# Gate block 6's negated half and adding DMA come first, and even heads of the indexer's last two row blocks take their PSUM bank from the values' pool

## The chip, the cores and the metric

The kernel runs on one core of a Trainium2 chip. The metric is the device time of one execution in microseconds (us). Before the change it was 752.59, 752.68 and 753.98 us in three runs, so the median is 752.68.

## The reference

The program computes one block of a streaming encoder for 512 frames of 1024 channels, in fp32. A projection feeds two attention branches with eight heads of 64 each; gates merge them; a layer norm, a gated feed-forward layer (width 2816, with a causal convolution of width 3) and a second layer norm follow.

```python
proj = x @ w_in
q_a, k_a, v_a, q_i, k_i, w_i, q_s, k_s, v_s, g_a, g_b = split(proj)

# branch A (heads a0..a7): an indexer picks the 128 best keys of a query
dots  = einsum('thd,sd->ths', q_i, k_i) * 64**-0.5        # 8 indexer heads, one key head
score = einsum('th,ths->ts', w_i, relu(dots))             # masked to earlier chunks
sel   = top_k(score, 128)                                 # 128 = min(256, 512 // 4)
y_a   = softmax(q_a . k_a[sel] / 8 + bias) @ v_a[sel]

# branch B (heads s0..s7): stick breaking, no softmax
log_beta, log_keep = log_sigmoid(z), log_sigmoid(-z)      # z = q_s . k_s / 8, causal
y_s   = exp(log_beta + sum of log_keep over later keys) @ v_s

merged = sigmoid(g_a + b_a) * (y_a @ w_dsa) + sigmoid(g_b + b_b) * (y_s @ w_sb)
x = layer_norm(alpha * x + merged @ w_out)
u, g = split(x @ w_ffn_in)
x = layer_norm(alpha * x + (gelu(conv(u)) * g) @ w_ffn_out)
```

## The kernel before, in words

**Products in three matmuls.** Each fp32 operand of a projection is split in a high half and a low half, and a product is the sum of three matmuls into one PSUM bank. In the projections (`proj_t`) these are the lines L230 (high weights, high x), L231 (high weights, low x) and L232 (low weights, high x). A projection of 128 output channels has 8 such triples, 24 matmuls of 128x512.

**The weight stream.** The class `Stream` brings the weights in the order in which the matmuls use them. SP's queue loads a raw block (128x1024, L72) a few blocks ahead; ACT writes the high half `whi` (L103); the low half `wlo` is raw minus high. For most blocks DVE or POOL subtracts (L110). For the fourteen blocks in `DMA_LO`, gate blocks gb0 to gb7 among them, ACT writes the *negated* high half into `wlo` (L106), and then a DMA that POOL issues reads the raw weights from memory a second time and adds them to it (L107). `whi` and `wlo` are rings of three blocks each, so that a block may be written only when the matmuls of the block three places earlier are done. The numbers in the names count the blocks: `wlo_29` belongs to gb5, `wlo_30` to gb6, `wlo_31` to gb7, `whi_32` to qa1.

**Filler and heads.** The list `FILL` is the order of the projections: ... qa0 ka0 gb4 gb5 gb6 gb7 qa1 ka1 va ... (q, k and v of the branches, gates of branch B). They are cut into triples and put between the steps of the attention heads, which have waits in them. The heads go s0 to s7, then a0 to a7. For an s head, TensorE forms z (L530), ACT takes the two sigmoids (L534 and L535, tiles `keep` and `beta`), DVE scans `keep` (L544), and POOL multiplies `beta` by the scan (`sb_sticks`, L547). Tiles `beta_1524`, `beta_1642` and `beta_1773` belong to heads 5, 6 and 7. The result has to be transposed before it meets the values. From head 4 on (`TURN = 4`) that is done by DMA: `send_planes` splits the fp32 words into two 16-bit planes (L466 on ACT, L467 on POOL), SP issues two transposing DMAs (L469), and `join_planes` puts the planes together (L478 on ACT, L479 on POOL) and writes high and low halves (`pth` L481 on ACT, `ptl` L485 on DVE). TensorE reads both in `weigh` (L501).

**The indexer.** `idx_scores` walks over row blocks 1, 2 and 3 (256, 384 and 512 keys) and eight heads in each: two matmuls into a PSUM tile `dot_ps` (L403, L404), a relu on ACT (L406), and on DVE a product with the head's weight that adds to the score (L409, L411). The selection (`select`, L420 and L421 on DVE) is a long row of rounds, dealt out between the later steps.

**PSUM.** There are two pools of four banks. `pa` serves the projections and the indexer's dots; `pb` serves the values' projection (`vs_ps0` to `vs_ps3`), and after it the heads.

**What sets the order.** Each engine runs its instructions in a fixed order. A scheduler, which times the program when it is built, sets that order; `tc.issue_after(x)` makes what is written under it come after x in that plan. Ahead of the change the multiply of head 5 (L547, `i == TURN + 1`) came after the last adding DMA written so far (`st.added`); the multiply of head 6 had no such tie.

## Time and profile before

| | |
|---|---|
| time, median of three runs | 752.68 us |
| the profiled execution | 753.88 us, of which the span of the trace is 752.1 us |
| granted TensorE clock over the span | 0.994 |
| PE (TensorE matmul) busy | 739.6 us, 98% |
| DVE (VectorE) busy | 569.3 us, 76% |
| ACT (ScalarE) busy | 406.4 us, 54% |
| POOL (GpSimd) busy | 149.5 us, 20% |
| queue 1 (transfers that SP's and ACT's queues issue) | 41.1% of 16 DMA engines' span |
| queue 0 (transfers that POOL issues) | 9.7% |

All times are microseconds from the start of the span. PE is the matrix engine's matmuls, PEld its weight loads, DVE the vector engine, ACT the scalar engine, POOL the GpSimd engine, SP the queue that issues most transfers. In a row of the timeline stand the start, the duration, the engine, the line, the operation and the tiles (out<-in, without numbers); in square brackets the time for which the engine stood idle before it, and what it waited for. Matmuls overlap: one is listed with 0.39 us, but the next starts 0.23 us after it. The clock column (PEclk) is the share of full speed that the chip granted to TensorE.

### The profile page before, as it was taken

The numbers are of one execution on the slowest core, as the hardware profiler recorded it, in microseconds if no ns is written. First come the engines' busy times: TensorE is split into PE (matmuls) and PEld (weight loads), VectorE is DVE, ScalarE is ACT, GpSimd is POOL, SyncE is SP. The second block draws the span as 40 slices with busy tenths as digits, with TensorE's granted clock in tenths as the row PEclk, the third lists the DMA queues.
The fourth block names the chain that finished last, engine by engine and source line by source line (L and its number), as shares of the span: only waits on it lengthen the run. The fifth ranks groups of instructions, "written<-read, shape, count | busy, mean of one in ns | idle before, by whom it ended". The sixth has DMA issues, their size and how long they took to land.

```text
span 752.1 us, 9760 instructions
## 1 busy us (share of the span) xinstructions
PE 739.6 (98%) x3485; PEld 619.5 (82%) x3485; DVE 569.3 (76%) x907; ACT 406.4 (54%) x572; POOL 149.5 (20%) x161
## 2 busy tenths in 40 slices
PE   9999999998999999999999999999999999999995
PEld 7877888886888888888889888888888888888885
DVE  5569788998579999658774967676776668668995
ACT  5465767795786588746374534443443344346430
POOL 1001224374742432000011111011101101110011
PEclk9999999999999999999999999999999999999998
DMA  8445887796556455327732444435343444448532
GB/s 268 151 127 183 190 183 170 151 203 162 133 152 161 122 146 118 121 61 231 303 60 75 170 143 158 146 114 167 125 159 136 140 141 143 141 146 290 198 117 84
DMA packets 71008, 116.38 MB, mean 155 GB/s; under 512 B 39913, under 2 KB 40169, under 8 KB 70961
## 3 DMA queue, kind: packets, MB, share of 16 engines
q1 hardware_dynamic: 63680, 93.33, 41.1%
q0 software_dynamic: 5744, 18.38, 9.7%
q10 hardware_dynamic: 1536, 4.06, 2.2%
q8 instruction: 27, 0.44, 0.3%
q14 instruction: 21, 0.16, 0.1%
HBM read 95.93 MB, written 9.98 MB: 141 GB/s over the span
## 4 chain that ended last, share of the span: by engine, by line
PE 92%; DVE 4%; DMA 1%; issue 1%; ACT 1%; POOL 0%; DVEq 0%; POOLq 0%; ACTq 0%
PE u_ps L922 5%; PE u_ps L921 5%; PE g_ps L922 5%; PE u_ps L923 5%; PE g_ps L921 5%; PE g_ps L923 5%; PE m L1002 2%; PE m L1001 2%; PE m L1003 2%; PE av_ps L501 2%; PE ga_ps L232 2%; PE ga_ps L231 2%; PE ga_ps L230 2%; PE o_ps L852 2%; PE o_ps L851 2%; PE o_ps L850 2%
## 5 line engine op out<-in xcount | busy, mean ns | idle before, releaser
L103 ACT ACTIVATE whi<-raw 128x1024 fp32r<-128x1024 f32 (+1 forms) x124 | 124.0, 1002 | 158.7 <-PE g_ps L922 45.9
L110 DVE TENSOR_TENSOR wlo<-raw,whi 128x1024 fp32r<-128x1024 f32 (+1 forms) x105 | 124.3, 1185 | 40.4 <-ACT whi L103 39.5
L923 PE MATMUL u_ps<-x1h,wlo 128*128 128x512 f32 (+1 forms) x192 | 71.4, 372 | 0.0
L921 PE MATMUL u_ps<-x1h,whi 128*128 128x512 f32 (+1 forms) x192 | 71.3, 372 | 0.0
L922 PE MATMUL u_ps<-x1l,whi 128*128 128x512 f32 (+1 forms) x192 | 71.3, 371 | 0.0
L921 PE MATMUL g_ps<-x1h,whi 128*128 128x512 f32 (+1 forms) x184 | 69.9, 380 | 0.0
L922 PE MATMUL g_ps<-x1l,whi 128*128 128x512 f32 (+1 forms) x184 | 69.9, 380 | 0.0
L923 PE MATMUL g_ps<-x1h,wlo 128*128 128x512 f32 (+1 forms) x184 | 69.9, 380 | 0.0
L921 PEld LDWEIGHTS u_ps<-x1h,whi 128*128 128x128 f32 x192 | 36.2, 188 | 6.3
L922 PEld LDWEIGHTS u_ps<-x1l,whi 128*128 128x128 f32 x192 | 36.2, 188 | 6.2
L923 PEld LDWEIGHTS u_ps<-x1h,wlo 128*128 128x128 f32 x192 | 36.2, 188 | 6.2
L921 PEld LDWEIGHTS g_ps<-x1h,whi 128*128 128x128 f32 x184 | 34.6, 188 | 6.6
L923 PEld LDWEIGHTS g_ps<-x1h,wlo 128*128 128x128 f32 x184 | 34.6, 188 | 6.5
L922 PEld LDWEIGHTS g_ps<-x1l,whi 128*128 128x128 f32 x184 | 34.6, 188 | 6.5
L944 DVE TENSOR_TENSOR t<-raw 128x512 f32<-128x512 f32 x11 | 7.6, 692 | 40.0 <-DMA raw<-in_w_fo_dram 39.6
L559 POOL TENSOR_TENSOR bm<-win,score 128x256 f32<-128x256 f32 (+2 forms) x24 | 26.0, 1112 | 32.2 <-DMA pl<-bm 16.1
L963 POOL MEMSET u<- 128x2 f32 x22 | 2.1, 98 | 145.0 <-ACT whi L103 101.2
L977 DVE TENSOR_TENSOR hF<-g_ps,c 128x512 f32<-128x512 f32 x22 | 15.1, 686 | 20.8 <-PE g_ps L923 20.8
L969 ACT ACTIVATE c<-c,cwt 128x512 f32<-128x512 f32 x22 | 15.9, 725 | 25.2 <-DVE c L968 25.0
L819 POOL TENSOR_TENSOR rstd<-rstd,mhalf 128x1 f32<-128x1 f32 x8 | 7.7, 958 | 104.4 <-DVE rstd L818 104.4
L232 PE MATMUL gb_ps<-xh,wlo 128*128 128x512 f32 x64 | 25.7, 404 | 2.6 <-DMA wlo<-in_w_t_dram 2.6
L420 DVE MAX8 m<-score 128x8 f32<-128x256 f32 (+2 forms) x48 | 26.5, 554 | 1.7 <-DMA pl<-keep 0.8
(578 smaller groups left out, 2085.2 us busy)
## 6 DMA issues: line engine op xcount, KB each, us to landing
raw<-in_w_fi_dram SPq DMA_DIRECT2D x44, 512.0 KB, 3.3
raw<-in_w_t_dram SPq DMA_DIRECT2D x32, 512.0 KB, 3.5
raw<-in_w_fo_dram SPq DMA_DIRECT2D x26, 512.0 KB, 4.1
wlo<-in_w_t_dram POOLq DMA_DIRECT2D x14, 512.0 KB, 7.1
raw<-in_w_br_dram SPq DMA_DIRECT2D x8, 512.0 KB, 4.0
raw<-in_w_o_dram SPq DMA_DIRECT2D x8, 512.0 KB, 4.4
raw<-in_w_v_dram SPq DMA_DIRECT2D x7, 512.0 KB, 3.8
raw_b<-in_w_fo_dram SPq DMA_DIRECT2D x6, 512.0 KB, 5.3
```

Source lines behind the costliest of these rows:

```text
L103: self.high = nc.scalar.activation(hi[:, :w], t[:, :w], AF.Copy).ins
L110: self.done[key] = eng.tensor_sub(lo[:, :w], t[:, :w], r32(hi[:, :w])).ins
L230: nc.tensor.matmul(ps[:M], wh[:, c], xh[k], start=(k == 0), stop=False)
L231: nc.tensor.matmul(ps[:M], wh[:, c], xl[k], start=False, stop=False)
L232: nc.tensor.matmul(ps[:M], wl[:, c], xh[k], start=False, stop=(k == KC - 1))
L420: nc.vector.max(m8, sc)
L559: nc.gpsimd.tensor_add(bm[:, OFF[j]:OFF[j] + N], win[:, 512 - N:512], score[j])
L921: nc.tensor.matmul(ps[:, c], wh[:, kc], x1h[:, k, c], start=(k == 0), stop=False)
L922: nc.tensor.matmul(ps[:, c], wh[:, kc], x1l[:, k, c], start=False, stop=False)
L923: nc.tensor.matmul(ps[:, c], wl[:, kc], x1h[:, k, c], start=False, stop=(k == KC - 1))
L969: nc.scalar.activation(c, c, AF.Gelu_apprx_tanh, bias=cwt[:, f, 3:4])
L977: nc.vector.tensor_mul(F[:, o:o + 2].rearrange("p a b -> p (a b)"), gps_, c)
```

## The change

1. For gb6 the negated half (L106) comes in ACT's order straight behind the block's high half. In the code, the high half of the next block, the two copies of ka0 (`stack_hl`, L335 and L336) and the sigmoid of gb4 (L627) are ordered behind it; ka0's copies had been ordered behind head 4's joined high half before.
2. The multiply of head 6 (L547) comes behind gb6's adding DMA in POOL's order; the one of head 5 comes behind gb5's, by name.
3. In row blocks 2 and 3 of the indexer, heads 0, 2, 4 and 6 take their PSUM bank from `pb`, the others from `pa` as before.

```diff
@@ -64,6 +64,7 @@
         self.loaded, self.split, self.used = {}, {}, 0
         self.nl = self.ns = 0
         self.high = self.behind = None
+        self.highs = {}
 
     def queue(self, dst, src):
 
@@ -103,8 +104,10 @@
                 self.high = nc.scalar.activation(hi[:, :w], t[:, :w], AF.Copy).ins
             self.behind = None
             if key in self.lo_by_dma:
-                self.high = nc.scalar.activation(lo[:, :w], r32(hi[:, :w]), AF.Copy, scale=-1.0).ins
-                self.done[key] = self.added = nc.gpsimd.dma_start(lo[:, :w], self.pieces[self.ns][1], accum_op=ALU.add).ins
+                self.high = self.highs[key] = nc.scalar.activation(lo[:, :w], r32(hi[:, :w]), AF.Copy, scale=-1.0).ins
+                if key == "gb6":
+                    self.behind = self.high
+                self.done[key] = nc.gpsimd.dma_start(lo[:, :w], self.pieces[self.ns][1], accum_op=ALU.add).ins
             else:
                 eng = nc.gpsimd if key in self.lo_on_pool else nc.vector
                 self.done[key] = eng.tensor_sub(lo[:, :w], t[:, :w], r32(hi[:, :w])).ins
@@ -398,7 +401,7 @@
             N = 128 * (j + 1)
             for h in range(H):
                 yield j
-                ps = pa("dot_ps")
+                ps = (pb if j > 1 and h % 2 == 0 else pa)("dot_ps")
                 r = slice(j * 128, j * 128 + 128)
                 nc.tensor.matmul(ps[:, :N], qi[h][:, r], kih[:, :N], start=True, stop=False)
                 nc.tensor.matmul(ps[:, :N], qi[h][:, r], kil[:, :N], start=False, stop=True)
@@ -535,7 +538,7 @@
             ups[h] = nc.scalar.activation(beta[:, c], ps[:, :o], AF.Sigmoid, scale=0.125).ins
         return beta, keep
 
-    def sb_sticks(beta, keep, behind=False):
+    def sb_sticks(beta, keep, behind=None):
 
         for j in (1, 0, 2, 3):
             N = 128 * (j + 1)
@@ -543,7 +546,7 @@
             rev = keep[:, hi:lo:-1]
             scan = nc.vector.tensor_tensor_scan(rev, rev, first[:, 512 - N:512][:, ::-1], 0.0, op0=ALU.mult,
                                                 op1=ALU.max)
-        with tc.issue_after(st.added) if behind else nullcontext():
+        with tc.issue_after(st.done[behind]) if behind else nullcontext():
             nc.gpsimd.tensor_mul(beta, beta, keep[:, 1:ATT + 1])
         return scan.ins
 
@@ -620,11 +623,12 @@
             if kind in ("qs", "qa"):
                 qk[t] = stack_dup(ps, 1.0 if kind == "qs" else -0.125, t)
             elif kind in ("ks", "ka"):
-                with tc.issue_after(firsts[0]) if t == "ka0" and firsts else nullcontext():
+                with tc.issue_after(st.highs["gb6"]) if t == "ka0" and firsts else nullcontext():
                     qk[t] = stack_hl(ps, "k", 4, t)
             elif kind == "gb":
                 g = xp.tile([128, 512], F32, tag="m", bufs=8, name=t)
-                ups[t] = nc.scalar.activation(g, ps, AF.Sigmoid, bias=bgt[:, 8 + n:9 + n]).ins
+                with tc.issue_after(st.highs["gb6"]) if n == 4 else nullcontext():
+                    ups[t] = nc.scalar.activation(g, ps, AF.Sigmoid, bias=bgt[:, 8 + n:9 + n]).ins
                 m.append(g)
             elif n >= EARLY:
                 gps[n] = ps
@@ -707,7 +711,7 @@
                 for ins in emptied["va"] if h == 2 else ends if h == 1 else ():
                     ties.enter_context(tc.issue_after(ins))
                 return following[0]()
-        last = sb_sticks(*following, behind=i == TURN + 1)
+        last = sb_sticks(*following, behind={TURN + 1: "gb5", TURN + 2: "gb6"}.get(i))
         if i < TURN:
             return following[0], last
         return send_planes(*following, nc.gpsimd), last
```

The scheduler makes a new order out of this. Lines of the changed kernel are one to four higher than those of before (L103 is L104, L106 is L107, L107 is L110, L335 is L338, L403 is L406, L466 and L467 are L469 and L470, L481 is L484, L547 is L550, L627 is L631).

ACT, where gb6's weights are split; `whi_30` and `wlo_30` are gb6's halves, `whi_31` and `wlo_31` gb7's, `ka0a` and `ka0b` the copies of ka0, `back_1718` the joined planes of head 5, `keep_1643` a plane of head 6. Before:

```order
L103 ACTIVATE whi_30_1624<-raw_30_1622 128x1024
L335 ACTIVATE ka0a_1676<-ka0_ps_1629 64x512
L336 ACTIVATE ka0b_1677<-ka0_ps_1629 64x512
L103 ACTIVATE whi_31_1684<-raw_31_1682 128x1024
L627 ACTIVATE gb4_1755<-gb4_ps_1689,bgt_105 128x512
L106 ACTIVATE wlo_30_1625<-whi_30_1624 128x1024
L106 ACTIVATE wlo_31_1685<-whi_31_1684 128x1024
L478 ACTIVATE back_1718<-pl_1574 128x1280
L466 ACTIVATE keep_1643<-beta_1642 128x1280
```

and with the change:

```order
L104 ACTIVATE whi_30_1624<-raw_30_1622 128x1024
L107 ACTIVATE wlo_30_1625<-whi_30_1624 128x1024
L338 ACTIVATE ka0a_1676<-ka0_ps_1629 64x512
L339 ACTIVATE ka0b_1677<-ka0_ps_1629 64x512
L104 ACTIVATE whi_31_1684<-raw_31_1682 128x1024
L631 ACTIVATE gb4_1755<-gb4_ps_1689,bgt_105 128x512
L107 ACTIVATE wlo_31_1685<-whi_31_1684 128x1024
L481 ACTIVATE back_1718<-pl_1574 128x1280
```

The negated half of gb6 has moved ahead of four instructions, among them gb7's high half; the plane of head 6 (`keep_1643`) has moved behind the sigmoids of head 7.

POOL, around the adding DMAs of gb6 and gb7 (`wlo_30`, `wlo_31`) and the multiplies of heads 6 and 7 (`beta_1642`, `beta_1773`). Before:

```order
L467 COPY keep_1525<-beta_1524 128x1280
L547 TENSOR_TENSOR beta_1642<-beta_1642,keep_1643 128x1280
L107 DMA wlo_30_1625<-in_w_t_dram 128x1024
L107 DMA wlo_31_1685<-in_w_t_dram 128x1024
L467 COPY keep_1643<-beta_1642 128x1280
L479 COPY back_1718<-pl_1574 128x1280
L547 TENSOR_TENSOR beta_1773<-beta_1773,keep_1774 128x1280
```

and with the change:

```order
L470 COPY keep_1525<-beta_1524 128x1280
L110 DMA wlo_30_1625<-in_w_t_dram 128x1024
L550 TENSOR_TENSOR beta_1642<-beta_1642,keep_1643 128x1280
L110 DMA wlo_31_1685<-in_w_t_dram 128x1024
L482 COPY back_1718<-pl_1574 128x1280
L470 COPY keep_1643<-beta_1642 128x1280
L550 TENSOR_TENSOR beta_1773<-beta_1773,keep_1774 128x1280
```

gb6's DMA now stands ahead of the multiply of head 6, gb7's still behind it, and the join of head 5 (`back_1718`) has passed the plane of head 6.

PE, from the last dots of row block 1 (`dot_ps_517` to `dot_ps_544`, 128x256) into row block 2 (128x384). Before, from the second matmul of head 4:

```order
L404 MATMUL dot_ps_517<-kil_445,qi2a_383 128x256
L403 MATMUL dot_ps_526<-kih_444,qi2b_384 128x256
L404 MATMUL dot_ps_526<-kil_445,qi2b_384 128x256
L403 MATMUL dot_ps_535<-kih_444,qi3a_389 128x256
L404 MATMUL dot_ps_535<-kil_445,qi3a_389 128x256
L403 MATMUL dot_ps_544<-kih_444,qi3b_390 128x256
L404 MATMUL dot_ps_544<-kil_445,qi3b_390 128x256
L403 MATMUL dot_ps_557<-kih_444,qi0a_371 128x384
L404 MATMUL dot_ps_557<-kil_445,qi0a_371 128x384
L403 MATMUL dot_ps_569<-kih_444,qi0b_372 128x384
L404 MATMUL dot_ps_569<-kil_445,qi0b_372 128x384
```

and with the change:

```order
L407 MATMUL dot_ps_517<-kil_445,qi2a_383 128x256
L406 MATMUL dot_ps_557<-kih_444,qi0a_371 128x384
L407 MATMUL dot_ps_557<-kil_445,qi0a_371 128x384
L406 MATMUL dot_ps_526<-kih_444,qi2b_384 128x256
L407 MATMUL dot_ps_526<-kil_445,qi2b_384 128x256
L406 MATMUL dot_ps_581<-kih_444,qi1a_377 128x384
L407 MATMUL dot_ps_581<-kil_445,qi1a_377 128x384
L406 MATMUL dot_ps_535<-kih_444,qi3a_389 128x256
L407 MATMUL dot_ps_535<-kil_445,qi3a_389 128x256
L406 MATMUL dot_ps_544<-kih_444,qi3b_390 128x256
L407 MATMUL dot_ps_544<-kil_445,qi3b_390 128x256
L406 MATMUL dot_ps_611<-kih_444,qi2a_383 128x384
```

Dots of row block 2 in banks of the values' pool (`dot_ps_557`, `dot_ps_581`, heads 0 and 2) now stand between those of row block 1. The same 40 dot matmuls, counted from the start of the program, lie ahead of the next projection (qs0) in both kernels.

PE again, where head 5's weights (`pth_1721`, `ptl_1722`) meet the values, `l_ps` are the logits of head a0. Before, the sixteenth matmul of qa1 and what follows:

```order
L230 MATMUL qa1_ps_1930<-xh5_302,whi_32_1759 128x512
L501 MATMUL av_ps_1808<-pth_1721,vs0_704 128x384
L570 MATMUL l_ps_1945<-ka0a_1676,qa0a_1616 128x512 x2
L570 MATMUL l_ps_1950<-ka0a_1676,qa0a_1616 128x128 x2
L570 MATMUL l_ps_1950<-ka0a_1676,qa0a_1616 128x384 x2
L570 MATMUL l_ps_1959<-ka0a_1676,qa0a_1616 128x256
L501 MATMUL av_ps_1808<-ptl_1722,vs0_704 128x384
```

and with the change, from the first matmul of qa1:

```order
L233 MATMUL qa1_ps_1930<-xh0_131,whi_32_1759 128x512
L504 MATMUL av_ps_1808<-pth_1721,vs0_704 128x384
L234 MATMUL qa1_ps_1930<-xl0_132,whi_32_1759 128x512
L235 MATMUL qa1_ps_1930<-xh0_131,wlo_32_1760 128x512
L573 MATMUL l_ps_1945<-ka0a_1676,qa0a_1616 128x512 x2
L573 MATMUL l_ps_1950<-ka0a_1676,qa0a_1616 128x128 x2
L573 MATMUL l_ps_1950<-ka0a_1676,qa0a_1616 128x384 x2
L573 MATMUL l_ps_1959<-ka0a_1676,qa0a_1616 128x256
L504 MATMUL av_ps_1808<-ptl_1722,vs0_704 128x384
```

The block has moved ahead of most of qa1. On DVE the low half it reads (`ptl_1722`) has moved too: behind `wlo_32` (qa1's low half) it now has one round of the selection ahead of it instead of three, and `wlo_33` (ka1's) no longer stands ahead of it.

## The prediction

> **What bounds the kernel now.** I read the profile's page first, then PE's waits, then the chain through the longest of them, then the timelines around it. Busy time and the list of what PE waited for:

> ```profile
> span 752.1 us, 9760 instructions
> PE 739.6 (98%) x3485; PEld 619.5 (82%) x3485; DVE 569.3 (76%) x907; ACT 406.4 (54%) x572; POOL 149.5 (20%) x161
> ...
> PE gb_ps L232 <- DMA wlo<-in_w_t_dram: 2.6, 1, 2.6
> PE idle_ps L207 <- DVE idle L204: 1.2, 1, 1.2
> PE dot_ps L403 <- ACT relu L406: 1.0, 1, 1.0
> ```

> PE is the bound, so only a hole in it, or a lowered clock, can be won. The change aims at two of its three holes. The chain through the first one (start, duration, what):

> ```profile
> 162.27 3.52 POOL beta L547
> ...
> 165.91 7.51 DMA wlo<-in_w_t_dram
> ...
> 173.46 0.80 PE gb_ps L232
> ```

> gb6's adding DMA left POOL only when head 6's multiply was done, and landed 7.51 us later. PE around it, and what ran at full rate later:

> ```profile
> 170.50 0.39 PE L231 MATMUL gb_ps<-xl,whi 128*128 128x512 f32 x1
> 173.46 0.80 PE L232 MATMUL gb_ps<-xh,wlo 128*128 128x512 f32 x1 [2.57 <-DMA wlo<-in_w_t_dram]
> ...
> 185.07 0.39 PE L230 MATMUL qa_ps<-xh,whi 128*128 128x512 f32 x1
> ...
> 188.47 0.40 PE L230 MATMUL qa_ps<-xh,whi 128*128 128x512 f32 x1
> ```

> The fifteen steps from 185.07 to 188.47 are 0.227 us each. So the L232 was due at 170.50 + 0.23 = 170.73 and came 2.73 late. From it to 185.07 there are 44 matmuls (22 left of gb6, 22 of gb7), 9.97 us at that step; they took 11.61. The missing 1.64 is the clock (us; PE, PEld, DVE, ACT, POOL busy; clock; DMA share; GB/s):

> ```profile
> 173.00:174.00 1.00, 0.54 (x1) 0.50 (x2) 1.00 (x2) 1.00 (x2) 0.00 (x0) 0.61 1.05 209
> 174.00:175.00 1.00, 1.00 (x4) 0.75 (x3) 1.00 (x3) 0.14 (x1) 0.00 (x0) 0.50 0.12 21
> 175.00:176.00 1.00, 1.00 (x4) 0.81 (x3) 1.00 (x4) 0.00 (x0) 0.00 (x0) 0.50 0.02 4
> 176.00:177.00 1.00, 1.00 (x4) 0.76 (x4) 1.00 (x2) 0.00 (x0) 0.37 (x1) 0.68 0.00 0
> ```

> Half clock makes up (0.39 + 0.50 + 0.50 + 0.32) = 1.71 us of lost time, some of it inside the hole: the two readings agree. The whole stall costs 2.73 + 1.64 = 4.37.

> [...] The rows above show half clock right behind that gap. If the clock had dropped for a reason of its own, the stall would be worth 2.73 alone and the sum below would end 1.6 higher, at 748.8; I follow the rows.

> **The change, part by part. gb6's supply.** ACT and POOL now (gb5's pair shows how fast a DMA can follow its negated half):

> ```profile
> 150.92 1.04 ACT L106 ACTIVATE wlo<-whi 128x1024 fp32r<-128x1024 f32 x1
> 160.73 1.04 ACT L103 ACTIVATE whi<-raw 128x1024 fp32r<-128x1024 f32 x1
> 161.68 0.57 ACT L335 ACTIVATE ka0a<-ka_ps 64x512 fp32r<-64x512 f32 x1
> 164.55 2.00 ACT L106 ACTIVATE wlo<-whi 128x1024 fp32r<-128x1024 f32 x2
> ...
> 152.26 0.88 POOL L107 DMA_DIRECT2D wlo<-in_w_t_dram  x1 [1.13 <-ACT wlo L106]
> 156.91 1.46 POOL L467 COPY keep<-beta 128x1280 uint16<-128x1280 uint16 x1
> 162.24 3.55 POOL L547 TENSOR_TENSOR beta<-beta,keep 128x1280 f32<-128x1280 f32 x1 [3.87 <-DVE keep L544]
> ...
> DMA to landing us min/median/max: 5.2/7.1/9.1
> ```

> The last row is the landing of all fourteen adding DMAs of L107; the 9.1 is gb7's, issued right behind gb6's.

> The negated half moves from 164.55 to 161.68, directly behind `whi` at 160.73, and ends about 162.73. gb5's DMA began 0.30 behind its half (152.26 against 151.96), so gb6's begins near 163.03; POOL is idle there, its copy ended at 158.37 and the multiply now stands behind the DMA. Landing: gb6's own 7.5 gives 170.5, inside the 170.73 that PE asks for; the ends are 168.2 (5.2) and 172.1 (9.1). I take 170.5, the same transfer three microseconds earlier: no hole, or a few tenths. The dots' hole of 1.0 us (below) left the clock alone, so I charge no clock for a short one. Gain 4.37. The bounds: 4.37 at the one end; at the other a landing at 172.1, which leaves a hole of 1.4 and a gain of 3.0, or of 1.3 if the clock falls for that too.

> **What is pushed back.** Head 6's multiply starts behind the DMA's 0.88 us, at about 163.9 instead of 162.24, and ends at 167.5 by its old 3.55. Queued behind it on POOL are gb7's DMA, the join of head 5 and head 6's plane; for the first waits PE (next), for the second head 5's block (below), for the third SP's transposes of head 6. ACT's four moved instructions each start 1.0 later, so gb7's negated half ends where it did (166.55) and its DMA goes at 167.5 instead of 166.8. It lands at 175.0 with 7.5, at 176.6 with its old 9.1, though a gap of four microseconds to gb6's DMA speaks for the lower figure. PE asks for it 22 matmuls behind 170.73, at 175.72: covered by 0.7 us, at worst a hole of 0.9. I take zero for it and 0.4 for both blocks together.

> **The dots.** PE and ACT at the third hole:

> ```profile
> 52.37 0.28 PE L404 MATMUL dot_ps<-kil,qi3b 128*128 128x256 f32 x1
> 53.66 0.44 PE L403 MATMUL dot_ps<-kih,qi0a 128*128 128x384 f32 x1 [1.01 <-ACT relu L406]
> 54.12 0.34 PE L403 MATMUL dot_ps<-kih,qi0b 128*128 128x384 f32 x1
> 54.30 0.34 PE L404 MATMUL dot_ps<-kil,qi0b 128*128 128x384 f32 x1
> 57.34 0.39 PE L403 MATMUL dot_ps<-kih,qi0b 128*128 128x512 f32 x1
> 59.12 0.50 PE L230 MATMUL qs_ps<-xh,whi 128*128 128x512 f32 x1
> 59.46 0.39 PE L231 MATMUL qs_ps<-xl,whi 128*128 128x512 f32 x1
> ...
> 55.02 2.50 ACT L406 ACTIVATE relu<-dot_ps 128x384 f32<-128x384 f32 x6 [0.20 <-PE dot_ps L404]
> 57.96 2.09 ACT L406 ACTIVATE relu<-dot_ps 128x384 f32<-128x384 f32 x4 [0.44 <-DVE score L411]
> ```

> From 52.37 to 59.46 lie the rest of one 256 step (0.12), sixteen of 384 (0.175), eight of 512 and one of qs0 (0.23): 4.99 us of work in 7.09, so 2.10 are lost, half as a hole and half as slow steps. The cause is the bank: with four banks qs0 needs the one of row block 3, head 0, four dots back. With even heads in the other pool it needs that of row block 2, head 5. On ACT's list this relu is the ninth behind head 3 of row block 1, that one the fourteenth; five relus at 2.50 / 6 = 0.42 are 2.1 us. I take 1.5, since some of it returns as shorter waits for relus; bounds 0 (if the relu that waited for DVE at 57.96 sets the pace) and 2.1.

> Does the lead last over 110 us? DVE waits for work that hangs on PE, between the dots and gb6:

> ```profile
> 108.69 1.62 DVE L451 TENSOR_TENSOR ptl<-tr_ps,pth 128x512 fp32r<-128x512 f32 x3 [2.38 <-ACT pth L450]
> 121.78 0.68 DVE L354 SCALAR_TENSOR_TENSOR qs3a<-qs_ps,qs3a 64x512 fp32r<-64x512 f32 x1 [1.76 <-ACT qs3a L353]
> ```

> So DVE was not saturated and comes earlier with PE; gb6's supply should move along. If it doesn't, 1.3 us come back at gb6 as a hole.

> **Head 5 at the end of the gates.** Its values block now comes behind one matmul of qa1 instead of sixteen:

> ```profile
> 178.31 0.68 DVE L421 MATCH_REPLACE8 score<-m,score 128x512 f32<-128x512 f32 x1
> 184.52 1.48 DVE L485 TENSOR_TENSOR ptl<-back,pth 128x1280 fp32r<-128x1280 f32 x1
> ...
> 188.70 0.34 PE L501 MATMUL av_ps<-pth,vs 128*128 128x384 f32 x1
> ...
> 190.03 0.34 PE L501 MATMUL av_ps<-ptl,vs 128*128 128x384 f32 x1
> ```

> PE reaches qa1 at 185.07 - 4.37 = 180.70 (times without the dots' lead). `ptl` is asked for after three qa1 matmuls (0.68) and the 1.33 from 188.70 to 190.03: at 182.7. On DVE it now follows the round that ended at 178.99, so it ends near 180.5: 2.2 us of cover. Without it, see the third rival. On SP the transposes of head 6 go ahead of two loads of va's weights:

> ```profile
> 182.94 3.61 SPq L469 DMA_TRANSPOSE pl<-keep  x2
> ```

> That makes those loads up to 3.6 us later. The second block of va is asked for behind qa1, ka1 and va's first block, 72 matmuls behind 180.70, so not before 197; I price it at zero, and so the planes of heads 6 and 7, which gain a place on one engine where they lose one on another. Each microsecond beyond that cover would be a hole in va.

> **Sum.** 752.1 - 4.4 - 1.5 + 0.4 = 746.6 of span. The profiled execution took 753.88, 1.8 above its span and 1.2 above the median of 752.68; so 746.6 + 1.8 - 1.2 = **747.2 us**.

> **The rivals.** *gb6 still lands late* (9.1 as gb7's, or the supply not moving with PE): for it speaks the spread of 5.2 to 9.1, against it that the 9.1 was the second of two DMAs in a row. A hole of 1.4 instead of 0.4 gives 748.2, with the clock 749.8. [...]

> *The dots give nothing*, because relu and score set the pace: 747.2 + 1.5 = 748.7. The 0.44 at 57.96 speaks for it, the nine relus in place of fourteen against.

> *A new hole at head 5*: if `ptl` stays where it was (186.0), PE waits 186.0 - 182.7 = 3.3 there and loses 1.6 of clock, 4.9 in all: 752.1, no change.

> *Slower*, by the same mechanism: the pushed multiply, join and planes delay `ptl` beyond its old time. The point is 0.6 us past 186.0, where the loss passes 5.5; with 3 us, 755. Its place is POOL's and ACT's list between 164 and 180, where the multiply starts 1.7 later than before. Against it: `ptl` has to become 5.5 us later than I reckon it (186.0 instead of 180.5) before the point is even reached.

> *That the change does not do what it says* is out for gb6 (the order of ACT and POOL has it) and is for the dots the second rival.

> **How the numbers follow.** Forecast 0.62 (746.2 to 748.2), late gb6 0.14, dots for nothing 0.09, new hole 0.08, slower 0.07. The forecast's low end is the dots at 2.1 and no residual, its high end a hole of 1.4. The range 745.6 to 750.6 holds the first three cases: 749.8, the highest of them, and 0.6 to 0.8 at either end for the scatter of runs (752.59 to 753.98 now). A measurement of this kernel tells 0.2%, 1.5 us, from no change: faster means under 751.2. That is 0.84 from the first three; 0.09 same; 0.07 slower.

> **What would show it.** Right: no wait for `wlo` at gb6's first L232, clock 1.00 from 170 to 177, qs0 about 1.5 us earlier, gb6's DMA near 161.5 (163.0 less the lead). Wrong: an L232 waiting for gb6 or gb7 over 1 us, qs0 at 59 as before, an L501 waiting for DVE's `ptl`, or a DVE that no longer follows PE between 60 and 160.

## The result, and the profile after

The changed kernel took 748.69 us, the median of five runs (748.38 to 749.85). The kernel before, run beside it on the same chip, took 753.98 (752.59 to 756.15, five runs). The ratio is 0.9928, with a 95% interval of 0.9907 to 0.9949: faster by 0.7%, or 5.3 us. The forecast was 747.2 us, 5.5 under the time before; the measured time is inside its range, 1.5 above the forecast.

The page of the changed kernel, with the span and the busy time of each engine:

```profile
span 746.3 us, 9766 instructions
PE 736.9 (99%) x3485; PEld 618.2 (83%) x3485; DVE 570.8 (76%) x907; ACT 406.7 (54%) x572; POOL 147.9 (20%) x161
```

And all that PE waited for in it (total, times, longest, in us):

```profile
PE idle_ps L210 <- DVE idle L207: 1.2, 1, 1.2
PE bs_ps L603 <- DVE ka2b L341: 0.4, 1, 0.4
PE bs_ps L605 <- DVE wlo L113: 0.2, 1, 0.2
```

The holes at gb6 and at the dots are gone. What is left beside the start-up (`idle_ps`) are two waits at `bs`, the projection of branch B's heads (`y_s @ w_sb`): 0.2 us some 58 us behind gb6 (L605) and 0.4 us some 86 us behind it (L603). Neither was there before.

gb6's supply in the timelines of ACT and POOL (start, duration; lines are three higher than before, so L107 is the negated half, L110 the adding DMA and L550 the multiply):

```profile
159.62 1.06 ACT L107 ACTIVATE wlo<-whi 128x1024 fp32r<-128x1024 f32 x1
...
160.98 0.87 POOL L110 DMA_DIRECT2D wlo<-in_w_t_dram  x1 [4.79 <-ACT wlo L107]
161.59 2.76 POOL L550 TENSOR_TENSOR beta<-beta,keep 128x1280 f32<-128x1280 f32 x1
164.80 0.88 POOL L110 DMA_DIRECT2D wlo<-in_w_t_dram  x1 [0.46 <-DMA pl<-keep]
```

The landing times stand in the view of L110's instructions, first for gb6's DMA alone and then for gb7's:

```profile
DMA to landing us min/median/max: 6.3/6.3/6.3
...
DMA to landing us min/median/max: 6.8/6.8/6.8
```

gb6's DMA now stands ahead of the multiply and goes 4.9 us earlier than in the profile before (165.91). It lands at 160.98 + 6.3 = 167.3. Here is PE at the same place, at the dots, and where gb7 ends:

```profile
53.32 0.44 PE L406 MATMUL dot_ps<-kih,qi0b 128*128 128x384 f32 x1
...
57.05 0.39 PE L233 MATMUL qs_ps<-xh,whi 128*128 128x512 f32 x1
...
167.62 0.40 PE L233 MATMUL gb_ps<-xh,whi 128*128 128x512 f32 x1
...
168.54 0.39 PE L235 MATMUL gb_ps<-xh,wlo 128*128 128x512 f32 x1
...
178.51 0.40 PE L233 MATMUL qa_ps<-xh,whi 128*128 128x512 f32 x1
178.74 0.34 PE L504 MATMUL av_ps<-pth,vs 128*128 128x384 f32 x1
179.38 1.32 PE L573 MATMUL l_ps<-ka0a,qa0a 128*128 128x512 f32 x7
180.54 0.34 PE L504 MATMUL av_ps<-ptl,vs 128*128 128x384 f32 x1
```

The first low-half matmul of gb6 (168.54) waits for nothing, with 1.2 us of cover. That margin is not always there: in the six profiles below that have the same order at gb6 (e2, e5 to e8, e12) the DMA lands after 6.3 to 7.5 us, and the cover goes from 1.3 us (e5) down to 0.1 (e6) and nothing (e12, where PE starts 0.04 us behind the landing). None of them has a hole there. qs0 begins at 57.05 instead of 59.12. qa1 begins at 178.51 instead of 185.07. The clock over these ten microseconds (us; PE, PEld, DVE, ACT, POOL busy; clock; DMA share; GB/s) stayed full:

```profile
170.00:180.00 10.00, 10.00 (x47) 8.29 (x46) 9.93 (x15) 5.95 (x7) 4.04 (x2) 1.00 0.64 137
```

**Lead** is the word used below for how much earlier PE reaches the same matmul than in the first profile of the kernel before, read from the two traces. Each column is a place, with its time in the profile before. The experiments ran on several chips; the ratio of each is against the kernel before on its own chip.

| kernel | 7, first `vs_ps` | 77, qs2 | 170, ahead of gb6's hole | 179, in gb7 | 220 | 300, behind `bs` | 508 |
|---|---|---|---|---|---|---|---|
| changed | .34 | 2.19 | 2.19 | 6.56 | 6.42 | 5.86 | 5.85 |
| changed, again (e8) | -.08 | 1.67 | 1.66 | 6.03 | 5.90 | 5.68 | 5.68 |
| before, again (e9) | .02 | -.05 | -.06 | -.34 | -.35 | -.55 | -.56 |
| before, again (e10) | -.06 | -.08 | -.08 | -.20 | -.20 | .13 | .13 |
| before, again (e11) | -.12 | -.17 | -.17 | .98 | .98 | -.63 | -.63 |
| e1, dots alone | -.69 | 1.15 | 1.15 | 2.19 | 2.19 | .24 | .24 |
| e2, gb6 alone | -.57 | -.66 | -.66 | 3.71 | 3.57 | 2.73 | -2.26 |
| e3, no tie for the multiply | .04 | 1.80 | 1.79 | 1.24 | 1.14 | 1.72 | 1.71 |
| e4, no early half | .59 | 2.44 | 2.43 | 2.16 | 2.13 | 2.67 | 2.66 |
| e5, e2 with another bank | .02 | -.06 | -.06 | 4.30 | 4.17 | 3.90 | 3.90 |
| e6, changed with that bank | -.48 | 1.37 | 1.36 | 5.62 | 5.49 | 5.17 | 5.16 |
| e7, dots of row block 2 alone | -.34 | .23 | .23 | 4.60 | 4.41 | 3.32 | 3.32 |
| e12, va2's low half on DVE | -.43 | 1.41 | 1.41 | 5.60 | 4.09 | 4.08 | 4.07 |

The first column is the scatter of the program's start and has nothing to do with the change; a gain is the difference of two columns. In the changed kernel the dots gave 2.19 - 0.34 = 1.85, gb6 gave 6.56 - 2.19 = 4.37, and 0.70 was given back by 300. The sum, 5.5, with the 0.3 of the start is the 5.8 between the spans (752.1 and 746.3).

### The profile page after: what moved, and what is told of

The parts are those of the page before. It is cut to its first block, busy times and chain, and to the rows that moved or that the text cites. A ratio compares the mean times of both kernels' runs of the same rounds, so it can differ in the third digit from the quotient of the medians.

```text
span 746.3 us, 9766 instructions
## 1 busy us (share of the span) xinstructions
PE 736.9 (99%) x3485; PEld 618.2 (83%) x3485; DVE 570.8 (76%) x907; ACT 406.7 (54%) x572; POOL 147.9 (20%) x161
## 4 chain that ended last, share of the span: by engine, by line
PE 89%; DVE 4%; issue 2%; ACT 2%; POOL 2%; DMA 1%; DVEq 0%; POOLq 0%; ACTq 0%
PE u_ps L927 5%; PE u_ps L925 5%; PE g_ps L927 5%; PE g_ps L925 5%; PE u_ps L926 5%; PE g_ps L926 5%; PE m L1006 2%; PE m L1007 2%; PE m L1005 2%; PE av_ps L504 2%; PE ga_ps L235 2%; PE ga_ps L234 2%; PE gb_ps L235 2%; PE gb_ps L234 2%; PE ga_ps L233 2%
## 5 line engine op out<-in xcount | busy, mean ns | idle before, releaser
L104 ACT ACTIVATE whi<-raw 128x1024 fp32r<-128x1024 f32 (+1 forms) x124 | 124.0, 1002 | 150.3 <-PE g_ps L926 46.0
L562 POOL TENSOR_TENSOR bm<-win,score 128x256 f32<-128x256 f32 (+2 forms) x24 | 26.2, 1119 | 33.9 <-DMA pl<-bm 29.1
L550 POOL TENSOR_TENSOR beta<-beta,keep 128x1280 f32<-128x1280 f32 x8 | 21.7, 2709 | 26.9 <-DVE keep L547 20.9
```

Source lines behind the costliest of these rows:

```text
L104: self.high = nc.scalar.activation(hi[:, :w], t[:, :w], AF.Copy).ins
L550: nc.gpsimd.tensor_mul(beta, beta, keep[:, 1:ATT + 1])
L562: nc.gpsimd.tensor_add(bm[:, OFF[j]:OFF[j] + N], win[:, 512 - N:512], score[j])
```

## The experiments

### e1: the dots alone

The kernel before with one line of the change:

```diff
-                ps = pa("dot_ps")
+                ps = (pb if j > 1 and h % 2 == 0 else pa)("dot_ps")
```

> Only the third part: the kernel before with even heads of row blocks 2 and 3 in the values' pool. Theory: qs0 starts 1.8 us earlier, the lead stays until gb6, and gb6's supply moves along with PE, so its stall (2.7 us of hole, 1.6 of clock) is as before: a span near 752.1 - 1.8 = 750.3. Rival, supply fixed in time: gb6's L232 starts at 173.4 as before, the hole grows by the lead, span near 752.1. Rival, no gain at the dots: qs0 within 0.5 of 59.1, span near 752.

Measured: 752.86 us (751.06 to 753.65), ratio 0.998 (0.9968 to 0.9992). PE's waits:

```profile
PE gb_ps L232 <- DMA wlo<-in_w_t_dram: 3.0, 1, 3.0
...
PE bs_ps L602 <- DVE wlo L110: 1.0, 1, 1.0
PE bs_ps L600 <- DVE ka2b L338: 0.8, 1, 0.8
```

Two rows of its timeline:

```profile
172.73 0.50 PE L232 MATMUL gb_ps<-xh,wlo 128*128 128x512 f32 x1 [2.99 <-DMA wlo<-in_w_t_dram]
...
260.14 0.47 PE L600 MATMUL bs_ps<-ys0h,whi 128*128 128x512 f32 x1 [0.77 <-DVE ka2b L338]
```

The dots gave 1.84 (columns 7 and 77 of the table), and the lead was still there when gb6's hole came; gb6's DMA left 1.16 us earlier than before (164.75 against 165.91), so the supply had moved with PE, and the hole was 0.4 longer because the landing took longer (PE went on 7.98 us behind the DMA's start, against 7.55 before). In this profile the clock stayed up behind the hole (1.00 in each microsecond from 171 to 179), which put the lead at 2.19. Most of that was lost at `bs`, where PE now waited 1.8 us. So the dots are worth 1.84 at their place, and in the old order less at the end: 0.93 in this profile (columns 7 and 508; 1.44 more than e11, where the clock stayed up too), 1.3 between the medians of the timed runs (752.86 against 754.13 for the kernel before). The expected span of 750.3 was missed: the profile has 751.9. The chain of waits shows what holds `bs` in this kernel (start, duration, what; the rows are the pieces of POOL, the transposing DMA and DVE):

```profile
196.65 0.25 POOL wlo L110
...
202.26 3.07 POOL bm L559 x3
...
207.41 3.94 DMA pl<-bm
...
237.06 5.90 DMA pl<-bm
...
259.30 0.70 DVE ka2b L338
260.00 0.14 issue
260.14 0.47 PE bs_ps L600
```

From 197 on the chain does not go through PE at all: a low half and additions on POOL, transposes, ACT and DVE, twice over, until `ka2b`. It is a second chain beside PE, and in the old order it is almost as long as PE's own.

### e2 and e5: gb6 alone, and an accident 240 us later

e2 is the changed kernel with the dots put back (`ps = pa("dot_ps")`).

> Only the first two parts, all dots in the projections' pool as before. Theory: no wait at gb6, clock 1.00 there, 4.4 us won at gb6 and some 0.5 to 0.7 given back behind it: span 748.2 to 748.5. Rival, the parts depend on each other (without the lead at the dots gb6's DMA lands too late): a hole of up to 1.4 us at gb6, span 749.5 or more.

Measured: 754.92 us (752.94 to 756.77), ratio 1.0004 (0.9989 to 1.002): no gain, and a span of 754.2 where 748.2 to 748.5 was expected. The wait at gb6 was gone and its 4.37 won, but PE had a new hole, in the feed-forward layer (here in its waits, and then in its timeline):

```profile
PE u_ps L925 <- DVE hF L981: 3.1, 1, 3.1
```

```profile
418.41 0.39 PE L927 MATMUL g_ps<-x1h,wlo 128*128 128x512 f32 x1
421.87 0.55 PE L925 MATMUL u_ps<-x1h,whi 128*128 128x512 f32 x1 [3.07 <-DVE hF L981]
```

Behind it the clock was at half rate again (0.50 of full from 422.18 to 425.60); together 5.0 us (the lead falls from 2.73 to -2.26). The instructions of that place stand in the same order as in the kernel before. What differs is which PSUM bank the third tile of a pool gets (bank 4 in the program before, bank 5 in e2): the pool hands out the bank that its plan takes to be free first, and with the times shifted by a few microseconds that changed. The `u_ps` that waits takes bank 4; in e2 that is the one which DVE empties with the second gated product (`hF`), in the kernel before one that ACT empties earlier.

e5 tests that. It is e2 with the two pools of the feed-forward layer opened in the other order (and closed so), which gives that tile another bank and changes nothing at gb6 or the dots:

```diff
+    psc, psC = open_pool("psC", space=PSUM, reuse_waits="tile")
...
-    psc, psC = open_pool("psC", space=PSUM, reuse_waits="tile")
```

> As the run with the first two parts alone, but the two PSUM pools of the feed-forward layer are opened in the other order, so that its first u_ps of 512 columns takes a bank that ACT empties and not one that the second gated product on DVE empties. Theory: the loss of 5 us near 422 is an accident of bank assignment and goes away, all else stays: span 748.5 to 749.5. Rival, DVE's lateness there comes from the earlier gb6: the hole stays, span 753 or more.

Measured: 750.31 us (749.19 to 753.34), ratio 0.9946 (0.9929 to 0.9963), span 748.0. The hole is gone (the lead is 3.90 behind `bs` and 3.90 at 508), and what gb6's part is worth alone can be read: 4.36 at its place, 3.9 at the end. So the 5 us of e2 were an accident of bank assignment, and no property of gb6's order.

### e6: the changed kernel with that bank

The same exchange of pools on the changed kernel, where I expected it to do harm.

> The whole change with the same swap of the two pools; here it gives the first u_ps the bank that DVE empties. Theory: a hole of about 3 us near 415 and up to 1.7 us of lowered clock behind it: span 746.3 + 3 to 5 = 749.3 to 751.3. Rival, the swap means nothing: 746.3 to 747.

Measured: 749.04 us (748.28 to 749.11), ratio 0.9922 (0.9897 to 0.9947). My expectation of 749.3 to 751.3 was missed: there is no hole. The tile now waits for the first gated product, which is early enough (DVE's timeline; PE asks for the bank at 416.19):

```profile
414.64 0.68 DVE L981 TENSOR_TENSOR hF<-g_ps,c 128x512 f32<-128x512 f32 x1
```

So the changed kernel owes nothing to a lucky bank: both assignments are free of the hole there.

### e3 and e4: the two halves of gb6's part

The change moves the negated half up on ACT, and ties the multiply behind the DMA on POOL. e3 is the changed kernel without the second, e4 the changed kernel without the first:

```diff
e3:
-        last = sb_sticks(*following, behind={TURN + 1: "gb5", TURN + 2: "gb6"}.get(i))
+        last = sb_sticks(*following, behind={TURN + 1: "gb5"}.get(i))
e4:
-                if key == "gb6":
-                    self.behind = self.high
...
-                with tc.issue_after(st.highs["gb6"]) if t == "ka0" and firsts else nullcontext():
+                with tc.issue_after(firsts[0]) if t == "ka0" and firsts else nullcontext():
...
-                with tc.issue_after(st.highs["gb6"]) if n == 4 else nullcontext():
+                with nullcontext():
```

> The changed kernel without the tie that puts head 6's multiply behind gb6's adding DMA: the negated half is early, the multiply goes first on POOL. Theory: the DMA waits for the multiply and leaves within 0.3 us of where it left before, counted from PE's first gb6 matmul, so hole and clock loss are back: 746.3 + 4.4 = 750.7 of span. Rival, the early half alone is enough: span 746.3 to 747.

Measured for e3: 750.8 us (748.82 to 752.53), ratio 0.9947 (0.9927 to 0.9967), span 750.4. ACT, POOL and PE in its timeline:

```profile
160.01 1.06 ACT L107 ACTIVATE wlo<-whi 128x1024 fp32r<-128x1024 f32 x1
...
160.46 3.56 POOL L550 TENSOR_TENSOR beta<-beta,keep 128x1280 f32<-128x1280 f32 x1 [3.87 <-DVE keep L547]
163.95 0.87 POOL L110 DMA_DIRECT2D wlo<-in_w_t_dram  x1
...
172.13 0.50 PE L235 MATMUL gb_ps<-xh,wlo 128*128 128x512 f32 x1 [3.04 <-DMA wlo<-in_w_t_dram]
```

The half is done at 161.07, but the multiply began at 160.46, and the DMA stands behind it until 163.95. The hole is 3.04.

> The changed kernel with ACT's order as before (gb6's negated half behind ka0, gb7's high half and gb4's sigmoid), but the multiply behind gb6's DMA. Theory: the DMA leaves when the half is written, about 165.7 in the times of before less the lead of 2.2, so the hole is as long as before (2.5 to 2.8 us, clock lost) and the multiply starts 4 us late on top: span 750.5 to 752. Rival, POOL's order alone is enough: 746.3 to 747.

Measured for e4: 751.24 us (749.46 to 752.2), ratio 0.9952 (0.9935 to 0.9969), span 749.3:

```profile
163.48 0.87 POOL L108 DMA_DIRECT2D wlo<-in_w_t_dram  x1 [7.54 <-ACT wlo L107]
...
171.28 0.80 PE L233 MATMUL gb_ps<-xh,wlo 128*128 128x512 f32 x1 [2.83 <-DMA wlo<-in_w_t_dram]
```

(In e4 the lines are one higher than before.) POOL is empty and waits 7.54 us for ACT; the DMA leaves at 163.48, half a microsecond earlier than in e3, but PE's lead is 0.6 larger too. The hole is 2.83. The span is below the expected 750.5 to 752. Neither part alone takes anything off the hole; the DMA needs both. In both profiles the clock fell to 0.50 at the hole (from 172.50 to 175.92 in e3, from 171.10 to 174.52 in e4). By their mean clock (0.996 or 0.997 against 0.995) three of e3's five timed executions and three of e4's six seem to have kept it, so by the medians the two are 3.3 and 2.9 us faster than the kernel before (754.13), more than these profiles show. Yet both kernels end with more than e1: e3 keeps its 1.7 and e4 has 2.1 (columns 7 and 508), while e1's 1.84 shrank to 0.9. Neither waits at `bs`.

### e7: how the dots' gain comes about

The changed kernel with only row block 2 on `pb`, not row block 3: `ps = (pb if j == 2 and h % 2 == 0 else pa)("dot_ps")`.

> The whole change, but only row block 2 of the dots borrows banks of the values' pool; row block 3 is in the projections' pool as before. Theory: qs0 then takes the bank of row block 3, head 0 again and has to wait for its relu, about five relus later than in the change: the first hole goes, qs0 starts near 58.0 instead of 57.05, span 746.3 + 0.5 to 1.2. Rival, only the hole of 1.0 us at row block 2 mattered: qs0 within 0.3 of 57.05.

Measured: 750.5 us (749.75 to 750.87), ratio 0.9943 (0.9923 to 0.9963), span 748.6. PE in the timeline:

```profile
58.42 0.50 PE L406 MATMUL dot_ps<-kih,qi1b 128*128 128x512 f32 x1 [0.69 <-ACT relu L409]
```

The old hole in row block 2 is gone, but a new one of 0.69 stands in row block 3, and the gain at qs2 is 0.57 instead of 1.85. The expectation had the cause right and the place wrong: PE waits at a dot (head 3 of row block 3) and not at qs0, which begins at 58.99 instead of near 58.0. The span is above the expected 746.8 to 747.5, with a wait of 1.06 at `bs` in it. So the gain does come from the reach of the banks: the number of dots between a tile and the next use of its bank sets how far PE can run ahead of the relus, and it is needed in both row blocks.

### e8 to e11: both kernels again

Profiles taken again, to see what of the table is scatter: the changed kernel (e8, timed too) and the kernel before three times.

> The changed kernel once more, beside the others on the same chip. Theory: no wait above 0.5 us in the projections, clock 1.00 around gb6, spans close together near 746.5, since no hole is left that can drop the clock; the kernel before spreads over 3 us because its hole sometimes costs clock and sometimes does not.

> The kernel before, profiled again, three times in all, to see what its hole at gb6 costs in clock. Theory: the clock falls or not by where the hole lies in a window of time that does not start with it, so with the same hole of 2.6 to 3.0 us some profiles show 1.7 us of lost time behind it (3.4 us at half clock) and some none, nothing in between. Rival, the length of the hole decides: every hole of 2.5 us and more shows the loss, as in the first profile.

> As the run before it: the hole near 2.7 us again, and behind it either 1.7 us of lost clock or none.

> As the two runs before it: the hole near 2.7 us again, and behind it either 1.7 us of lost clock or none.

e8 took 749.02 us (748.55 to 749.64), ratio 0.9924 (0.9899 to 0.995), span 746.4. The kernel before had spans of 752.7, 752.0 and 752.8, and holes at gb6 of 2.73, 2.82 and 2.92 us. In the first two the clock fell to 0.50 as before (from 174.66 in e9, from 173.32 in e10). In the third it did not, as its windows show (PE, PEld, DVE, ACT, POOL busy; clock; DMA share; GB/s):

```profile
174.00:175.00 1.00, 1.00 (x4) 0.84 (x5) 1.00 (x3) 0.36 (x1) 0.00 (x0) 1.00 0.45 86
175.00:176.00 1.00, 1.00 (x6) 0.82 (x5) 1.00 (x3) 0.00 (x0) 0.00 (x0) 1.00 0.10 20
```

And among its waits stand these:

```profile
PE bs_ps L602 <- DVE wlo L110: 0.9, 1, 0.9
PE bs_ps L600 <- DVE ka2b L338: 0.7, 1, 0.7
```

With the clock kept, this kernel was 1.15 ahead behind gb6, and lost 1.61 at `bs`, by the same wait as e1's.

### e12: the wait that is left

The changed kernel has 0.6 us of waiting at `bs`. The smaller part (L605, 0.2 us) is for a low half on DVE. I took va2's low half from POOL, one of the engines of the second chain, and gave it to DVE:

```diff
-POOL_LO = "ks1 va0 va1 va2 va3".split()
+POOL_LO = "ks1 va0 va1 va3".split()
```

> The whole change, and the low half of the third block of va is made by DVE, no longer by POOL, where it stood ahead of the additions (L562) of head a1. Theory: the second chain (POOL's additions, ACT, DVE, the transposing DMA) that PE meets at the bs projections near 226 and 254 comes about 2 us earlier, the waits of 0.2 and 0.4 us there go, and the 0.4 to 0.7 us that the change gives back behind gb6 become 0 to 0.2: span 745.7 to 746.2. Rival, DVE itself is the limit there and its 1.2 us more make the waits longer: span 747 or more.

Measured: 748.06 us (747.26 to 750.2), ratio 0.9915 (0.9894 to 0.9936), which overlaps the change's own interval. The profiled execution had a span of 748.1, by far the longest of the six; the others had 745.1 to 746.1, about what was expected (745.7 to 746.2). DVE and PE in its timeline:

```profile
198.29 1.78 DVE L113 TENSOR_TENSOR wlo<-raw,whi 128x1024 fp32r<-128x1024 f32 x1 [2.04 <-ACT whi L104]
...
201.63 0.47 PE L270 MATMUL va_ps<-whi,xh 128*128 128x512 f32 x1 [1.06 <-DVE ka1b L341]
```

What is left of its waits at `bs`:

```profile
PE bs_ps L603 <- DVE ka2b L341: 0.3, 1, 0.3
```

The wait for the low half at `bs` is gone, the one for `ka2b` is not, and PE has a new one of 1.06 in va, because the subtraction that DVE was given stands ahead of ka1's copies. Whether this change gains anything is not decided: the interval does not tell it from the change, and the only trace is of the slowest execution, which need not show what the others waited for.

## Why the prediction was right, step by step

**gb6's stall, 4.37.** Right, mechanism and size: 4.37 in the changed kernel, 4.36 and 4.37 in e5 and e8, 4.37 in e2. No hole was left, where 0.4 had been charged for both gate blocks. The terms inside it were less exact. The DMA left at 160.98 where 161.5 was forecast. It landed after 6.3 where 7.5 was assumed; in e6 and e12 it did take 7.5, and PE then had next to no cover, as forecast (0.2). gb7 is asked for 22 matmuls behind 168.54, at 173.53, and lands at 164.80 + 6.8 = 171.6: 1.9 of cover where I had 0.7. The multiply took 2.76 and not 3.55, so nothing behind it on POOL was late. In the profile before, a DVE subtraction of 128x1280 (L485, 162.01 for 1.47) lay beside its first 1.24 us; in the changed kernel that subtraction ends at 161.30, ahead of it.

**The clock inside that stall, 1.64.** The size was right each time the clock fell, but it does not fall each time (below). In the two profiles of old order where it stayed up, e1 and e11, most of the time came back at `bs`. Over 48 timed executions of the kernel before, 31 with a mean clock of 0.996 or more had spans of 752.0 on average and the other 17 of 753.7, so on average the drop seems to cost about its 1.7 (the mean clock also counts the start and the end of the span, so the split is rough). How much of it is on the path when the second chain is as late as in e11, stays open.

**The dots, 1.5.** The mechanism was right (e7), the size too small: 1.75 to 1.85 in e1, e3, e4, e6, e8, e12 and the changed kernel. The term was taken 0.6 below its upper bound of 2.1, because some of the gain should return as shorter waits for relus; 0.25 to 0.35 returned.

**The lead lasts.** Right up to gb6: the columns 77 and 170 agree within 0.01 in all kernels. Wrong beyond: I asked only whether DVE follows PE between the dots and gb6, and not what PE meets next. Between 179 and 300 the changed kernel gave back 0.70, e8 0.35, e6 0.45, e5 0.40; with other orders it was more (e2 0.98, e7 1.28). This is the term that was missing from the sum; at 0.35 to 0.70 in the changed kernel it stands where the residual of 0.4 stood for another reason, so that the sum came out right partly by luck: (4.37 + 1.85 - 0.70) is 5.5, as (4.4 + 1.5 - 0.4) is.

**What was priced at zero.** Head 5's values block (the place of the third rival) had 2.2 of cover by the forecast. On the chip (DVE's timeline):

```profile
176.40 2.37 DVE L488 TENSOR_TENSOR ptl<-back,pth 128x1280 fp32r<-128x1280 f32 x1
```

`ptl` was ready at 178.77 and asked for at 180.54: 1.8. It took 2.37 instead of 1.48. POOL's multiply of the next head (173.46 for 3.95) ran beside its first 1.01 us, and the one other long subtraction of this kind in the changed kernel (189.74 for 2.60) had POOL's work beside it too; that this made them longer is not shown, though: in the profile before, the same subtraction of head 4 (162.01) took 1.47 with 1.24 us of head 6's multiply beside it, and there the multiply was the longer one, 3.55 (2.44 to 2.47 for those of heads 1 to 4). No rival came in: gb6 did not land late, the dots gave their gain, and nothing waited at head 5.

But the price of zero for the moved blocks missed a *gain*. In the new orders head 5's block and the first logits (`l_ps`) stand behind three matmuls of qa1 (nine in e4) instead of sixteen, and the second chain comes earlier. The end of that chain is `ka2b`, for which `bs` waits:

| kernel | first `l_ps` | `ka2b` begins |
|---|---|---|
| old order: before, e9, e10, e11 | 188.88, 189.23, 189.07, 187.89 | 259.5, 260.1, 259.4, 260.2 |
| old order, e1 | 186.69 | 259.3 |
| e3, e4 | 185.89, 185.13 | 254.2, 255.8 |
| new order without the dots, e2, e5 | 182.23, 181.63 | 256.8, 255.7 |
| new order, changed, e8, e6 | 179.38, 179.91, 180.31 | 253.7, 253.9, 254.4 |
| new order, e7, e12 | 181.34, 180.34 | 256.1, 255.5 |

In the old order `ka2b` stays between 259.3 and 260.2, whatever lead PE has: a lead of 2.2 (e1) moved it by 0.2. In every new order it is 2.5 to 6.5 us earlier. So had the hole at gb6 been taken away and nothing else moved, I would expect by this table that most of the 4.37 had been lost at `bs`, as most of e1's and e11's gains were; no run shows it. That the second chain moved up as well is shown; which of the moved blocks did it is not. The place of the first logits alone does not explain it (in e3 they come 0.8 earlier than in e1, `ka2b` 5.1), e3 and e4, with different orders, both have it, and no run undid the blocks' place alone.

**The sum.** Forecast 746.6 of span; measured 746.3 to 747.7 over the five runs, with a median of 746.6, and 746.4 in e8's profile. The 1.5 us by which the time is off lie in the step from span to time. The forecast added 1.8 and took off 1.2, because the profiled execution (753.88) was that much above the median of three runs. In the five runs of the changed kernel the time is 2.1 above the span, and over five runs the median of the kernel before is 753.98: the profiled execution was not a slow one.

## What to carry to other kernels

A late transfer has to be followed through every queue it stands in: here the half on ACT and the place on POOL each took nothing off the hole alone (e3, e4), and together up to 4.4 us, 1.6 of which hang on the clock. A lead on the busiest engine should be followed to the end of the program, not to the end of the changed stage: look for the next place where a second chain is nearly as long, because that decides how much is kept (1.84 won at the dots, 0.9 to 1.4 of it kept in e1). And when one part of a change seems to be worth nothing, compare the lead place by place before believing it: in e2 a bank that a planner dealt out otherwise, 240 us later, hid a gain of 4.4.

## What the runs showed of the hardware

**At the eight longest holes the clock cost 1.71 us or nothing.** They stand here by length, with the time lost to the clock at them (one less the granted clock, summed over time):

| hole | idle, us | of it in one step of the grid below, us | lost to the clock, us |
|---|---|---|---|
| before | 2.57 | 2.33 | 1.71 |
| e9 (before) | 2.73 | 2.42 | 1.71 |
| e10 (before) | 2.82 | 2.36 | 1.71 |
| e4 | 2.83 | 2.65 | 1.71 |
| e11 (before) | 2.92 | 1.55 | 0 |
| e1 | 2.99 | 1.81 | 0 |
| e3 | 3.04 | 3.03 | 1.71 |
| e2, feed-forward layer | 3.07 | 3.07 | 1.71 |

The loss is 1.71 or nothing: 3.41 us at half clock, or none. It does not go by length: the shortest hole had it, and two longer ones of 2.92 and 2.99 did not. The hole of 1.0 us at the dots did not have it: in the profile before the clock stays at 1.00 from 50 to 63, and in e9 to e11 the eight steps of 384 columns next behind it take 0.17 to 0.18 us each.

**gb7's adding DMA landed later when it left right behind gb6's.** When gb6's and gb7's were issued about 1 us apart (before, e1, e3, e9 to e11), they landed after 7.5 to 8.1 and 9.1 to 9.4 us; with 3.8 us between them (the changed kernel, e2, e5 to e8, e12), after 6.3 to 7.5 and 6.7 to 7.5 (e4, with 3.0 us: 7.8 and 7.7). For gb7's the first two ranges are far apart. For gb6's they meet, and the other adding DMAs of these kernels, 4 us or more from the next, land after 5.0 to 8.8 us, so that what the neighbour does to the first of the two stays open.
